# Two compressions taken in turn with projections, and half of an output projection held back over a change of halves

## The chip, the cores and the metric
The kernel runs on one core of a Trainium2 chip. The metric is the device time of one execution in microseconds (us). In the texts PE is TensorE, DVE is VectorE, ACT is ScalarE, POOL is GpSimd and SP is SyncE, whose queue issues the DMAs.

## The reference, cut to what matters
One decoder layer over 1024 tokens of width 1024, in float32. After an RMS norm one projection gives inputs for two mixers, whose outputs are concatenated, projected and added to x. A SwiGLU network (width 2816) and a last norm follow.
```python
z = h @ w_in
a_conv, q, kc_r, vc_r, ks, vs, kw, vw, g = jnp.split(z, splits, axis=-1)
conv_out = conv_mixer(a_conv, ...)          # gate, causal depthwise conv of width 31, norm, silu
kc = compress(kc_r, cmp_k_pe, cmp_k_w1, cmp_k_w2)
vc = compress(vc_r, cmp_v_pe, cmp_v_w1, cmp_v_w2)
nsa_out = nsa_attention(q, kc, vc, ks, vs, kw, vw, gates)   # compressed, chosen and window branch
x = x + jnp.concatenate([conv_out, nsa_out], -1) @ w_out
...
# compress: 32 rows of 64 make one block (stride 16), through w1 (2048 x 256), silu, w2 (256 x 64)
```

## The kernel before
Every product keeps float32 accuracy with three passes: each operand is split into a high part (cast to float32r) and a low part (the rest), and high x high, high x low and low x high are summed. `load_w` brings 512 KB of weights (DMA to `raw`, two buffers), lets ACT cast the high part and makes the low part in four pieces on POOL, or in one on DVE where it is called with `dve`; three buffers each hold high and low parts. `Feed` calls such loads two ahead of the one in use. `split` makes high and low of a result with ACT and DVE.

The order of the work is written by hand with generators. A generator yields estimated PE time after each product (0.216 a product of 512 columns, 0.117 to 0.12 of 264 or 274), and other generators are due by that time:

- The first part (`Drive`) runs over the first half of the tokens (0 to 511): `conv_in`, `compress_in` of the keys (two chunks of columns), q0 and q1 (`project_d`), `compress` of the keys (four chunks of `w1`, 24 products each), q2 to q5, `values` for the window branch, `compress_in` of the values, kw0 and ks0, `compress` of the values, kw1, `compress_v`, ks1. Beside it run side generators: `late_rows` (norm and transposes of row tiles 4 to 7), `tables` on POOL, `taps_in` (62 conv taps on DVE, two a step), `conv_tail`, and `stages_in(g)` (two compressed-attention stages `cmp_stage` for each of four groups, whose gaps are 5.0, 0.7, 10.0 and 0). `acc_bank` takes the banks of PSUM in turn by the string in `turn[1]`. `drive.run` takes the first FIRST_B = 48 items of the fill, and `drive.rest` issues what the sides still have.
- Then `weave` puts attention (main) and a fill together: for each unit of main, `RATIO_B` units of fill in the first half of attention (query tiles 0 to 3) and `RATIO_C` = 1.6 in the second. The fill `fill_b` holds the projections of the second half of the tokens, conv's last; then comes the output projection of set 0 in two parts (`kq`, each 512 rows of the mixed width, read back from `mix_d`), the norm, and products of the SwiGLU network (`ffn`). A yield of LEAD_C = 8 or MIXLAT = 6 gives the fill nothing to issue for that long; -1 means that it waits for main. `mixed(0, kq)` tells when attention has written that part.
- At last `second` does the output projection of set 1 (`out_proj_k`), beside more fill, and the remaining `ffn` passes end the program.

Instructions of one engine run in order, in an order that the framework makes of the traced one.

Of the kernel before, what the change touches and what calls it, by code (L numbers as in the profile page):

```python
# [19 lines left out]
P = 128  # L20
# [39 lines left out]


SLOPES = _slopes(HEADS)
RATIO_B = 0.9
RATIO_C = 1.6
RATIO_D = 1.3
LEAD_C = 8.0
# [22 lines left out]
def tile_hymba(ctx: ExitStack, tc, x, attn_norm, w_in, conv_w, conv_b, conv_ln_g, conv_ln_b,  # L89
# [186 lines left out]
    def win_chunk(c0):  # L276
        return load_w([(0, w_in[0, :, c0:c0 + P])], KT, P)
# [66 lines left out]
    def late_rows():  # L344
        for t in range(4, 8):
            with tc.issue_after(rows_in[0].ins), tc.issue_after(rows_in[1].ins):
                late[:] = [norm_rows(xts[t], xts[t], grow, pa, a4("junk"))]
            yield 2.4
            transpose_tile(xts[t], hhi[1], hlo[1], (t % 4) * P)

    rows = a4("rows")[:, :P]
# [76 lines left out]
            for i, z in ((0, zh), (1, zl)):  # L428
                sp.dma_start(dst[i, row:row + P, hf * 512:(hf + 1) * 512], z.bitcast(F32))

    def compress_in(ws, pe_col, out):
        xh = pa.tile([P, 8, GROUPS, 68], F32R, tag="xc", name="xh", bufs=2)
        xl = pa.tile([P, 8, GROUPS, 68], F32R, tag="xc", name="xl", bufs=2)
        for X in (xh, xl):
            pool.memset(X[:, :, :, 64:68].bitcast(F32), 0.0)
        for s in range(2):
            split(xh[:, :, 0, 64 + s], xl[:, :, 0, 64 + s], cols[:, pe_col + 8 * s:pe_col + 8 * s + 8])
        for hf in range(2):
            for m in range(2):
# [12 lines left out]
    def compress(xh, xl, w1, w2, tag, out):  # L452
        w1f = w1[0].rearrange("l d h -> (l d) h")
        hs = [bank("h0", tag), bank("h1", tag)]
        n = 0
        for jc in range(4):
            wh, wl = load_w([(0, w1f[jc * 512:(jc + 1) * 512, :])], 4, 256, dve)
            if jc == 1:
                w2r = pa.tile([P, 2, HD], F32, tag="w2r", name="w2r")
                pool.tensor_copy(w2r[:, 0, 0:1], wh[:, 0, 0:1].bitcast(F32))  # L460
            for j4 in range(4):
                j, s = (jc * 4 + j4) % 8, jc // 2
                for a, b in ((wh, xh), (wl, xh), (wh, xl)):
                    for ht in range(2):
                        mm(hs[ht][:, :264], a[:, j4, ht * P:(ht + 1) * P], b[:, j, :, s:s + 66],
                           start=n < 2, stop=n >= 94)
# [411 lines left out]
    def taps_in(n):  # L878
        taps = conv_taps(0)
        for _ in taps:  # L880
            yield n

    drive = Drive()
    xk, xv, kk, kv = [], [], [], []
    turn[1] = ACCS1
    drive.side(late_rows())
    drive.run(conv_in(first, 0))
    drive.side(tables(late[0], 3.0))
    drive.side(taps_in(2.2))
    drive.run(compress_in([win_chunk(C_KC + m * P) for m in range(2)], 68, xk))  # L890
    feed = Feed([q_load(m) for m in range(2)])
    for m in range(2):
        drive.run(project_d(feed, q_d, m * P, (0,), True))
    drive.run(compress(*xk, cmp_k_w1, cmp_k_w2, "s", kk))
    turn[1] = ACCS2
    feed = Feed([q_load(m) for m in range(2, 6)])
    for m in range(2, 6):
        drive.run(project_d(feed, q_d, m * P, (0,), True))
        if m == 2:
            compress_k(*kk)  # L900
            drive.side(stages_in(0), drive.t + 4.0)
        if m == 5:
            drive.side(stages_in(1))
    drive.run(values(Feed(value_loads(C_VW, 18)), 18, vw_d, 0))
    drive.side(stages_in(2))
    drive.run(compress_in([win_chunk(C_VC + m * P) for m in range(2)], 84, xv))
    drive.side(conv_tail(0))
    feed = Feed(kv_loads())
    for dst in (kw_d, ks_d):
        drive.run(project_d(feed, dst, 0, (0,)))  # L910
    drive.side(stages_in(3))
    drive.run(compress(*xv, cmp_v_w1, cmp_v_w2, "z", kv))
    turn[0] = -1
    for dst in (kw_d, ks_d):
        drive.run(project_d(feed, dst, P, (0,)))
        if dst is kw_d:
            compress_v(*kv)
    p2_stack.close()
    pa_stack.close()

# [80 lines left out]
    def set_in(si, p):  # L1001
        acts[si] = p
        pairs = [p.tile([P, 2, DM], F32, tag="x1", name="x1", bufs=2) for _ in range(2)]
        x1s[si] = [pairs[j // 2][:, j % 2, :] for j in range(4)]
        for t, x1 in zip(SETS[si], x1s[si]):
            sp.dma_start(x1, x[0, t * P:(t + 1) * P, :])

    def set_norm(si, p):
        pools[si] = p
        h2[si] = [[p.tile([P, 4, 512], F32R, name=f"h2_{si}_{w}_{j}") for j in range(2)] for w in range(2)]  # L1010
# [5 lines left out]
    def mix_in(si, kq):  # L1016
        assert mixed(si, kq)
        t0, n = SETS[si][0] * P, len(SETS[si]) * P
        mix = [acts[si].tile([P, 4, n], F32R, tag="act", name="mix", bufs=2) for _ in range(2)]
        for w in range(2):  # L1020
            sp.dma_start(mix[w].bitcast(F32),
                         mix_d[w, kq * 512:(kq + 1) * 512, t0:t0 + n].rearrange("(k p) t -> p k t", p=P))
        return mix

    def out_proj(feed, si, tags, kqs):
        for kq in kqs:
            mix = mix_in(si, kq)
            yield MIXLAT
            for ch in range(2):
                ws = [feed.get(), feed.get(1)]  # L1030
                for t, x1 in enumerate(x1s[si]):
                    o = bank("wo", tags[t % len(tags)])
                    n = 0
                    for k in range(4):
                        wh, wl = ws[k // 2]
                        for a, b in ((0, wh), (0, wl), (1, wh)):
                            pe.matmul(o, mix[a][:, k, t * P:(t + 1) * P], b[:, k % 2, :], start=n == 0, stop=n == 11)  # L1037
                            n += 1
                            yield MM
                    xs = x1[:, ch * 512:(ch + 1) * 512]  # L1040
                    dve.tensor_tensor(xs, o, xs, op=ALU.add)


    def out_proj_k(feed, si, tags):
        for kq in range(2):
            mix = mix_in(si, kq)
            feed.ahead(feed.n + 2)
            yield 0.0 if kq == 0 else MIXLAT
            for ch in range(2):
                os = [bank("wo", tags[t % len(tags)]) for t in range(len(x1s[si]))]  # L1050
# [100 lines left out]

    def fill_all():
        yield from fill_b()
        for kq in range(2):
            while not mixed(0, kq):
                yield -1.0
            if kq == 0:
                set_in(0, pm)
            else:
                p1_stack.close()  # L1160
                last["p3"], p = open_pool("p3", "left")
                set_norm(0, p)
            yield LEAD_C
            yield from out_proj(feed, 0, "z", (kq,))
        yield from ffn_norm_in(0, "z")
        while early[0] >= 0 and early[0] < NF // 2:
            early[0] += 1
            yield from ffn(feed, (0,), "z")
# [71 lines left out]
```

## Time and profile before
| | us |
|---|---|
| median of 3 runs (lowest to highest) | 1520.09 (1519.88 to 1520.77) |
| the profiled execution | 1518.21 |
| its span, first to last instruction | 1516.5 |
| PE, DVE, ACT, POOL busy in it | 1450.9, 824.9, 721.0, 816.6 |

Durations come from the profiled execution, whose span is its time less what lies around it. Busy is the time in which an engine has an instruction running; matmuls overlap, so that the sum of their durations is more than PE's busy time.

### The profile page before, as it was taken

To read this page: it belongs to the slowest core of one execution; us is meant where nothing else is said; L and a number is where in the kernel's file an instruction comes from. 1 tells how busy PE (TensorE), PEld (TensorE's weight loads), DVE (VectorE), ACT (ScalarE), POOL (GpSimd) and SP (SyncE) were. 2 spreads that over 40 slices of the span, in tenths; PEclk is the share of its full clock that TensorE was granted. 3 is DMA by queue.
4 is the path that set the end of the run, shared out by engine and by line. 5 is a ranking of instruction groups with operands and counts; after the bars stand their busy time and mean duration, and the time that the engine had idled before them with its cause. 6 is when DMAs were issued, how large, how long until landed. Compare 5 with 4: busy or idle time off the path is not lost.

```text
span 1516.5 us, 21864 instructions
## 1 busy us (share of the span) xinstructions
PE 1450.9 (96%) x7271; PEld 1217.2 (80%) x7271; DVE 824.9 (54%) x1936; ACT 721.0 (48%) x1468; POOL 816.6 (54%) x1156
## 2 busy tenths in 40 slices
PE   7989989999889889999999999999999999999997
PEld 6778779877768778888888877878788888888886
DVE  6994654667677686776677764223325222222323
ACT  6235655767766476666665654123212222222223
POOL 5626534757576455655664656445532545555554
PEclk9999999999999999999999999999999999999999
DMA  7237567666486362353353225433222322333332
GB/s 239 72 109 209 163 190 213 182 185 190 111 275 181 107 154 76 84 135 92 91 138 97 60 76 171 160 126 104 84 83 97 110 85 89 106 94 93 93 96 84
DMA packets 228717, 193.61 MB, mean 128 GB/s; under 512 B 15496, under 2 KB 197612, under 8 KB 228604
## 3 DMA queue, kind: packets, MB, share of 16 engines
q1 hardware_dynamic: 228604, 192.21, 43.0%
q8 instruction: 58, 0.95, 0.3%
q14 instruction: 55, 0.45, 0.1%
HBM read 158.42 MB, written 33.75 MB: 127 GB/s over the span
## 4 chain that ended last, share of the span: by engine, by line
PE 81%; DVE 7%; DMA 5%; ACT 4%; issue 2%; POOL 1%; SPq 0%; DVEq 0%; POOLq 0%; ACTq 0%
PE gu L1094 31%; PE dn L1114 15%; PE pt L783 5%; PE zo L145 4%; PE wo L1037 3%; PE vo L145 3%; PE wo L1055 3%; DVE cacc L553 3%; PE o L801 3%; DMA w_raw<-in_w_in_dram 2%; PE o L800 2%; PE s L756 2%; PE h L145 2%; DMA mix<-mix_d 1%; PE s L760 1%
## 5 line engine op out<-in xcount | busy, mean ns | idle before, releaser
L229 POOL TENSOR_TENSOR w_lo<-w_raw,w_hi 128x256 fp32r<-128x256 f32 (+1 forms) x688 | 526.8, 800 | 382.8 <-ACT w_hi L225 373.8
L1094 PE MATMUL gu<-h,w_hi 128*128 128x512 f32 x1408 | 454.4, 396 | 0.1
L225 ACT CAST w_hi<-w_raw 128x1024 fp32r<-128x1024 f32 (+1 forms) x182 | 190.4, 1050 | 389.6 <-PE gu L1094 166.9
L1094 PEld LDWEIGHTS gu<-h,w_hi 128*128 128x128 f32 x1408 | 263.1, 188 | 57.7 <-DVE h L233 0.4
L1094 PE MATMUL gu<-h,w_lo 128*128 128x512 f32 x704 | 278.8, 396 | 0.0
L1114 PE MATMUL dn<-w_hi,aw 128*128 128x512 f32 x704 | 234.8, 398 | 4.9 <-DVE af L1101 1.8
L777 POOL TENSOR_SCALAR pr<-pr,l,gates 128x640 f32<-128x640 f32 (+5 forms) x192 | 150.2, 798 | 125.0 <-DVE l L772 97.4
L1101 DVE TENSOR_TENSOR af<-gu,af 128x512 f32<-128x512 f32 x44 | 30.3, 690 | 287.4 <-PE gu L1094 204.9
L767 ACT ACTIVATE pr<-pr,m 128x640 f32<-128x640 f32 (+5 forms) x192 | 141.5, 738 | 93.5 <-DVE m L764 84.3
L1119 DVE TENSOR_TENSOR x<-dn,x 128x512 f32<-128x512 f32 x176 | 114.3, 684 | 94.2 <-PE dn L1114 93.9
L1114 PEld LDWEIGHTS dn<-w_hi,aw 128*128 128x128 f32 x704 | 131.8, 188 | 37.6 <-DVE af L1101 3.3
L233 DVE TENSOR_TENSOR pl<-pt,ph 128x384 fp32r<-128x384 f32 x264 | 141.7, 551 | 37.1 <-ACT ph L233 35.1
L1094 PEld LDWEIGHTS gu<-h,w_lo 128*128 128x128 f32 x704 | 132.2, 188 | 28.8
L233 ACT CAST ph<-pt 128x384 fp32r<-128x384 f32 x264 | 119.3, 478 | 74.6 <-PE pt L783 65.0
L783 PE MATMUL pt<-ident,pr 128*128 128x128 f32 x792 | 135.9, 276 | 3.3 <-DVE pl L233 2.5
L1114 PE MATMUL dn<-w_lo,aw 128*128 128x512 f32 x352 | 138.6, 394 | 0.0
L764 DVE CUSTOM_DVE_ANT_0 pr<-s,base 128x384 f32<-128x384 f32 (+3 forms) x192 | 101.4, 533 | 48.3 <-PE s L760 35.7
L783 PEld LDWEIGHTS pt<-ident,pr 128*128 128x128 f32 x792 | 102.3, 142 | 19.2 <-issue 2.6
L145 PE MATMUL zo<-h,w_hi 128*128 128x512 f32 x320 | 105.8, 400 | 4.0 <-ACT w_hi L225 2.6
L756 PE MATMUL s<-kt,q 128*128 128x384 f32 (+3 forms) x288 | 101.2, 353 | 1.5 <-DVE m L764 0.7
L800 PE MATMUL o<-ph,vt 128*128 128x384 f32 x264 | 98.3, 372 | 1.4 <-ACT ph L233 1.3
L801 PE MATMUL o<-pl,vt 128*128 128x384 f32 x264 | 93.4, 354 | 4.0 <-DVE pl L233 4.0
(207 smaller groups left out, 2320.9 us busy)
## 6 DMA issues: line engine op xcount, KB each, us to landing
w_raw<-in_w_gate_up_dram SPq DMA_DIRECT2D x84, 512.0 KB, 3.9
w_raw<-in_w_down_dram SPq DMA_DIRECT2D x42, 512.0 KB, 3.3
w_raw<-in_w_in_dram SPq DMA_DIRECT2D x40, 512.0 KB, 4.6
mix<-mix_d SPq DMA_DIRECT2D x8, 1024.0 KB, 6.7
q<-q_d SPq DMA_DIRECT2D x80, 96.0 KB, 3.1
qc<-q_d SPq DMA_DIRECT2D x32, 192.0 KB, 4.2
pc_d<-pct SPq DMA_DIRECT2D x16, 384.0 KB, 3.8
pct<-pc_d SPq DMA_DIRECT2D x32, 192.0 KB, 3.4
```

The source lines that it names most:

```text
L145: lastpe[0] = pe.matmul(*args, **kw)
L225: act.copy(hi[:, :n], raw[:, :n])
L229: eng.tensor_sub(lo[:, q], raw[:, q], hi[:, q].bitcast(F32))
L233: return act.copy(hi, src), dve.tensor_sub(lo, src, hi.bitcast(F32))
L756: pe.matmul(sv, q2[:, 0, r, :], kk_[:, 0, kk], start=True, stop=False)
L767: act.activation(pr[:, :n], pr[:, :n], AF.Exp, bias=m, scale=-1.0, accum_out=l3[:, r:r + 1])
L777: pool.tensor_scalar(x_, x_, l3[:, r2:r2 + 1], gates[:, i, c:c + 1], op0=ALU.mult, op1=ALU.mult)
L783: pe.transpose(pt[:, r * P:(r + 1) * P], prs[st][1 + r][:, kk * P:(kk + 1) * P], ident)
L800: pe.matmul(o[:, :384], v, ph, start=False, stop=False)
L801: pe.matmul(o[:, :384], v, pl, start=False, stop=last)
L1094: pe.matmul(o, w[:, k, :], h2[si][h][k // 4][:, k % 4, :], start=n == 0, stop=n == 3 * KT - 1)
L1114: pe.matmul(o, aws[si][:, a, k, t * P:(t + 1) * P], b[:, 0, ch * 512:(ch + 1) * 512], start=n == 0, stop=n == 5)
```

## The change
Eight things are edited. (1) One feed, `first`, serves the whole first part. (2) `compress` takes its chunks from that feed, with low parts on POOL instead of DVE. (3) The order is: `compress_in` of the keys, `values`, `compress` of the keys with q0 to q3 in turn after each chunk, q4, `compress_k`, q5, `compress_in` of the values, kw0, `compress` of the values with ks0 and kw1 after its first two chunks, ks1, `compress_v`. (4) Stages 0 to 3 start after q4, after `compress_in` of the values, after kw0 and after `compress` of the values; the sums of the projections from there on take "t" banks. (5) `late_rows` yields 4.0 instead of 2.4, `taps_in` 2.7 instead of 2.2. (6) RATIO_B is 0.82 instead of 0.9. (7) The output projection of set 0 asks for `mix` before the rows of x, in six pieces; of its first part the second half of the columns (48 products) is done after the second part's `mix` has been asked for. (8) In `out_proj_k` the loads of `mix` come in pieces too, and the x rows after them, in halves.
```diff
-RATIO_B = 0.9
+RATIO_B = 0.82
...
-            yield 2.4
+            yield 4.0
             transpose_tile(xts[t], hhi[1], hlo[1], (t % 4) * P)
...
-    def compress_in(ws, pe_col, out):
+    def compress_in(feed, pe_col, out):
+        ws = [feed.get(), feed.get(1)]
...
-            wh, wl = load_w([(0, w1f[jc * 512:(jc + 1) * 512, :])], 4, 256, dve)
+            wh, wl = feed.get()
...
+    def in_turn(main, others, part):
+        others = iter(others)
+        for n, d in enumerate(main):
+            yield d
+            if n % part == part - 1:
+                yield from next(others, ())
+        for o in others:
+            yield from o
...
+    def mixed_in(a, b):
+        return [ld for pair in itertools.zip_longest(a, b) for ld in pair if ld]
+
+    kvl = kv_loads()
+    first.loads += ([lambda m=m: win_chunk(C_KC + m * P) for m in range(2)] + value_loads(C_VW, 18)
+                    + mixed_in(w1_loads(cmp_k_w1), [q_load(m) for m in range(4)]) + [q_load(4), q_load(5)]
+                    + [lambda m=m: win_chunk(C_VC + m * P) for m in range(2)] + kvl[:1]
+                    + mixed_in(w1_loads(cmp_v_w1), kvl[1:3]) + kvl[3:])
...
-    drive.side(taps_in(2.2))
-    drive.run(compress_in([win_chunk(C_KC + m * P) for m in range(2)], 68, xk))
...
+    drive.side(taps_in(2.7))
+    drive.run(compress_in(first, 68, xk))
+    drive.run(values(first, 18, vw_d, 0))
+    drive.run(in_turn(compress(*xk, first, cmp_k_w2, "s", kk),
+                      [project_d(first, q_d, m * P, (0,), True) for m in range(4)], 24))
     turn[1] = ACCS2
...
+    drive.run(project_d(first, q_d, 4 * P, (0,), True))
+    compress_k(*kk)
+    drive.side(stages_in(0), drive.t + 4.0)
+    drive.run(project_d(first, q_d, 5 * P, (0,), True))
+    drive.run(compress_in(first, 84, xv))
+    drive.side(stages_in(1))
+    drive.run(project_d(first, kw_d, 0, (0,)))
+    drive.side(conv_tail(0), drive.t + 10.0)
     drive.side(stages_in(2))
...
+    turn[1] = "t"
+    drive.run(in_turn(compress(*xv, first, cmp_v_w2, "z", kv),
+                      [project_d(first, dst, r, (0,)) for dst, r in ((ks_d, 0), (kw_d, P))], 24))
     drive.side(stages_in(3))
...
+    drive.run(project_d(first, ks_d, P, (0,)))
+    compress_v(*kv)
...
-        for w in range(2):
-            sp.dma_start(mix[w].bitcast(F32),
-                         mix_d[w, kq * 512:(kq + 1) * 512, t0:t0 + n].rearrange("(k p) t -> p k t", p=P))
+        mix = [p.tile([P, 4, n], F32R, tag=tag, name="mix", bufs=2) for _ in range(2)]
+        src = [mix_d[w, kq * 512:(kq + 1) * 512, t0:t0 + n].rearrange("(k p) t -> p k t", p=P) for w in range(2)]
+        for a, b in ((0, 1), (1, 2), (2, 4)):
+            for w in range(2):
+                if tokens:
+                    sp.dma_start(mix[w][:, :, a * P:b * P].bitcast(F32), src[w][:, :, a * P:b * P])
+                else:
+                    sp.dma_start(mix[w][:, a:b, :].bitcast(F32), src[w][:, a:b, :])
...
-            mix = mix_in(si, kq)
+            mix = mix_in(si, kq, acts[si], tokens=False)
             feed.ahead(feed.n + 2)
+            if kq == 0:
+                x_in(si, 0)
+                x_in(si, 1)
...
-        for kq in range(2):
-            while not mixed(0, kq):
-                yield -1.0
-            if kq == 0:
-                set_in(0, pm)
-            else:
-                p1_stack.close()
-                last["p3"], p = open_pool("p3", "left")
-                set_norm(0, p)
-            yield LEAD_C
-            yield from out_proj(feed, 0, "z", (kq,))
+        while not mixed(0, 0):
+            yield -1.0
+        mix = mix_in(0, 0, pm)
+        set_in(0, pm)
+        x_in(0, 0)
+        x_in(0, 1)
+        yield LEAD_C
+        yield from out_proj(feed, 0, "z", mix, 0)
+
+        while not mixed(0, 1):
+            yield -1.0
+        p1_stack.close()
+        last["p3"], p = open_pool("p3", "left")
+        mix2 = mix_in(0, 1, p, "h21")
+        yield from out_proj(feed, 0, "z", mix, 1)
+        yield MIXLAT
+        for ch in range(2):
+            yield from out_proj(feed, 0, "z", mix2, ch)
+        set_norm(0, p)
```

## Rows read from the trace of the kernel before
**Rows 1.** Busy time by stretches: us, then each engine's busy time and instructions, clock, DMA.
```profile
core 0: us, PE busy (x) PEld busy (x) DVE busy (x) ACT busy (x) POOL busy (x), PEclk, DMA share, GB/s
58.00:91.00 33.00, 33.00 (x144) 26.68 (x143) 32.39 (x50) 9.82 (x19) 12.13 (x12) 1.00 0.18 50
91.00:104.00 13.00, 7.38 (x34) 6.60 (x33) 11.49 (x18) 3.33 (x7) 0.00 (x0) 0.74 0.54 177
104.00:187.00 83.00, 83.00 (x465) 72.06 (x464) 50.18 (x118) 47.20 (x133) 47.03 (x63) 1.00 0.63 181
187.00:229.00 42.00, 35.07 (x211) 30.60 (x209) 23.55 (x53) 23.99 (x55) 14.65 (x20) 0.96 0.62 185
326.00:429.00 103.00, 89.75 (x483) 74.40 (x484) 74.00 (x265) 76.85 (x216) 65.65 (x106) 0.97 0.61 170
429.00:448.00 19.00, 15.40 (x70) 12.63 (x69) 13.45 (x43) 12.14 (x44) 12.07 (x19) 0.91 0.98 340
478.00:504.00 26.00, 21.29 (x122) 18.14 (x121) 17.81 (x61) 16.63 (x37) 13.03 (x17) 0.93 0.69 201
560.00:1517.00 957.00, 941.78 (x4456) 777.87 (x4454) 435.31 (x898) 387.01 (x628) 506.13 (x689) 1.00 0.34 101
```
**Rows 2.** PE's timeline: start, length, instruction, idle before it and what ended that.
```profile
40.59 1.98 PE L248 MATMUL tp<-ident,xt 128*128 128x128 f32 x12 [2.85 <-DVE h L233]
...
96.91 0.81 PE L145 MATMUL h<-xh,w_hi 128*128 128x264 f32 x2 [5.08 <-ACT xh L233]
...
189.13 0.68 PE L145 MATMUL h<-xh,w_hi 128*128 128x264 f32 x2 [1.59 <-ACT w_hi L225]
...
437.83 0.76 PE L1037 MATMUL wo<-w_hi,mix 128*128 128x512 f32 x1 [3.16 <-DMA mix<-mix_d]
...
499.09 0.69 PE L1037 MATMUL wo<-w_hi,mix 128*128 128x512 f32 x1 [4.31 <-DMA mix<-mix_d]
```
**Rows 3.** Busy time by stretches at half clock, the longest and a short one.
```profile
96.50:103.30 6.80, 5.84 (x25) 5.54 (x26) 6.07 (x10) 1.98 (x3) 0.00 (x0) 0.50 0.53 178
499.20:502.60 3.40, 3.40 (x11) 2.83 (x12) 0.82 (x4) 0.48 (x1) 0.00 (x0) 0.51 1.06 298
```
**Rows 4.** The chain of waits in order of time: start, length, piece.
```profile
112.49 6.26 PE zo L145 x27
...
136.19 5.11 PE vo L145 x40
...
429.82 7.87 DMA mix<-mix_d
...
491.65 7.40 DMA mix<-mix_d
```
**Rows 5.** Groups of instructions in 58 to 104: busy us, mean ns, idle before.
```profile
L553 DVE SCALAR_TENSOR_TENSOR cacc<-y,cols,cacc 128x512 f32<-128x512 f32 x41 | 32.4, 819 | 0.3
...
L229 POOL TENSOR_TENSOR w_lo<-w_raw,w_hi 128x256 fp32r<-128x256 f32 x9 | 10.9, 1233 | 13.1 <-ACT w_hi L225 13.1
...
L233 ACT CAST xh<-zc 64x256 fp32r<-64x256 f32 x16 | 5.9, 367 | 24.7 <-DVE xl L233 20.3 <-PE zc L145 4.4
L229 DVE TENSOR_TENSOR w_lo<-w_raw,w_hi 128x1024 fp32r<-128x1024 f32 x3 | 3.6, 1212 | 0.0
```
**Rows 6.** POOL's timeline: a chunk's four pieces beside conv taps, and without.
```profile
79.54 5.62 POOL L229 TENSOR_TENSOR w_lo<-w_raw,w_hi 128x256 fp32r<-128x256 f32 x4 [13.15 <-ACT w_hi L225]
...
170.80 2.82 POOL L229 TENSOR_TENSOR w_lo<-w_raw,w_hi 128x256 fp32r<-128x256 f32 x4 [2.98 <-ACT w_hi L225]
```
**Rows 7.** DMA issues by kind: count, KB each, median us to landing.
```profile
w_raw<-in_w_in_dram SPq DMA_DIRECT2D x40, 512.0 KB, 4.6
```
**Rows 8.** Who PE waited for in 326 to 429: us, times, longest.
```profile
PE cv L145 <- ACT w_hi L225: 5.1, 3, 2.6
```
**Rows 9.** DVE's timeline: a row multiply, and conv taps.
```profile
32.01 7.28 DVE L241 SCALAR_TENSOR_TENSOR xt<-xt,rs,grow 128x1024 f32<-128x1024 f32 x1
...
62.23 6.69 DVE L553 SCALAR_TENSOR_TENSOR cacc<-y,cols,cacc 128x512 f32<-128x512 f32 x7
...
72.86 1.40 DVE L553 SCALAR_TENSOR_TENSOR cacc<-y,cols,cacc 128x512 f32<-128x512 f32 x2
```

More of the change, by code (lines that the diff above doesn't have):

```diff
@@ L450, in compress_in, with compress @@
         out.extend((xh, xl))
-    def compress(xh, xl, w1, w2, tag, out):
-        w1f = w1[0].rearrange("l d h -> (l d) h")
+    def compress(xh, xl, feed, w2, tag, out):
         hs = [bank("h0", tag), bank("h1", tag)]
@@ L881, in taps_in, with w1_loads @@
             yield n
+    def in_turn(main, others, part):
[6 more added lines that the diff above has]
+            yield from o
+    def w1_loads(w1):
+        w1f = w1[0].rearrange("l d h -> (l d) h")
+        return [lambda jc=jc: load_w([(0, w1f[jc * 512:(jc + 1) * 512, :])], 4, 256) for jc in range(4)]
+    def mixed_in(a, b):
[5 more added lines that the diff above has]
+                    + mixed_in(w1_loads(cmp_v_w1), kvl[1:3]) + kvl[3:])
     drive = Drive()
@@ L888, in tile_hymba @@
     drive.side(tables(late[0], 3.0))
-    drive.side(taps_in(2.2))
-    drive.run(compress_in([win_chunk(C_KC + m * P) for m in range(2)], 68, xk))
[L891 to L894, printed above, removed]
-    turn[1] = ACCS2
[L896 to L904, printed above, removed]
-    drive.side(stages_in(2))
[L906 to L910, printed above, removed]
-    drive.side(stages_in(3))
[L912 to L917, printed above, removed]
+    drive.side(taps_in(2.7))
[3 more added lines that the diff above has]
+                      [project_d(first, q_d, m * P, (0,), True) for m in range(4)], 24))
+    turn[1] = ACCS2
+    drive.run(project_d(first, q_d, 4 * P, (0,), True))
[6 more added lines that the diff above has]
+    drive.side(conv_tail(0), drive.t + 10.0)
+    drive.side(stages_in(2))
+    turn[1] = "t"
+    drive.run(in_turn(compress(*xv, first, cmp_v_w2, "z", kv),
+                      [project_d(first, dst, r, (0,)) for dst, r in ((ks_d, 0), (kw_d, P))], 24))
+    drive.side(stages_in(3))
+    drive.run(project_d(first, ks_d, P, (0,)))
+    compress_v(*kv)
     p2_stack.close()
@@ L1004, in set_in, with x_in @@
         x1s[si] = [pairs[j // 2][:, j % 2, :] for j in range(4)]
+    def x_in(si, ch):
+        h = slice(ch * 512, (ch + 1) * 512)
         for t, x1 in zip(SETS[si], x1s[si]):
-            sp.dma_start(x1, x[0, t * P:(t + 1) * P, :])
+            sp.dma_start(x1[:, h], x[0, t * P:(t + 1) * P, h])
     def set_norm(si, p):
         pools[si] = p
-        h2[si] = [[p.tile([P, 4, 512], F32R, name=f"h2_{si}_{w}_{j}") for j in range(2)] for w in range(2)]
+        h2[si] = [[p.tile([P, 4, 512], F32R, tag=f"h2{w}", name="h2", bufs=2) for _ in range(2)] for w in range(2)]
@@ L1013, in mixed, with mix_in @@
     def mixed(si, kq):
         return ("conv", si) in done and all(("mix", g, i) in done for g in range((2, GROUPS)[kq]) for i in SETS[si])
-    def mix_in(si, kq):
+    def mix_in(si, kq, p, tag="act", tokens=True):
         assert mixed(si, kq)
         t0, n = SETS[si][0] * P, len(SETS[si]) * P
-        mix = [acts[si].tile([P, 4, n], F32R, tag="act", name="mix", bufs=2) for _ in range(2)]
-        for w in range(2):
-            sp.dma_start(mix[w].bitcast(F32),
-                         mix_d[w, kq * 512:(kq + 1) * 512, t0:t0 + n].rearrange("(k p) t -> p k t", p=P))
-        return mix
@@ L1025, in out_proj @@
-    def out_proj(feed, si, tags, kqs):
-        for kq in kqs:
-            mix = mix_in(si, kq)
[L1028 to L1041, printed above, removed]
+        mix = [p.tile([P, 4, n], F32R, tag=tag, name="mix", bufs=2) for _ in range(2)]
@@ new lines, in mix_in, with out_proj @@
+        src = [mix_d[w, kq * 512:(kq + 1) * 512, t0:t0 + n].rearrange("(k p) t -> p k t", p=P) for w in range(2)]
[5 more added lines that the diff above has]
+                    sp.dma_start(mix[w][:, a:b, :].bitcast(F32), src[w][:, a:b, :])
+        return mix
+    def out_proj(feed, si, tags, mix, ch):
+        ws = [feed.get(), feed.get(1)]
+        for t, x1 in enumerate(x1s[si]):
+            o = bank("wo", tags[t % len(tags)])
+            n = 0
+            for k in range(4):
+                wh, wl = ws[k // 2]
+                for a, b in ((0, wh), (0, wl), (1, wh)):
+                    pe.matmul(o, mix[a][:, k, t * P:(t + 1) * P], b[:, k % 2, :], start=n == 0, stop=n == 11)
+                    n += 1
+                    yield MM
+            xs = x1[:, ch * 512:(ch + 1) * 512]
+            dve.tensor_tensor(xs, o, xs, op=ALU.add)
@@ L1044, in out_proj_k @@
     def out_proj_k(feed, si, tags):
         for kq in range(2):
-            mix = mix_in(si, kq)
+            mix = mix_in(si, kq, acts[si], tokens=False)
             feed.ahead(feed.n + 2)
+            if kq == 0:
+                x_in(si, 0)
+                x_in(si, 1)
             yield 0.0 if kq == 0 else MIXLAT
```

## The prediction
> **What bounds the kernel now.** I read the table by stretches first [rows 1]: TensorE (PE) is busy nearly all the time, every other engine far less, and the diff does not change PE's work. So the time can move only through PE's idle stretches (window minus busy) and through stretches at a lower clock. From 560 us to the end 957 us hold only 15 us of idle time, while 91 to 104 hold 5.62, 187 to 229 hold 6.93, 326 to 429 hold 13.25, 429 to 448 hold 3.60 and 478 to 504 hold 4.71. Next I asked PE's timeline what ended the long ones [rows 2]: a transpose waits for VectorE (DVE) at 40.59; the key compression for its input at 96.91; the value compression for a weight cast at 189.13 (the first of six short waits up to 204); the output projection twice for `mix`, 3.16 and 4.31 us. Last the granted clock [rows 3]: after idle like these it is at half, the lower of its two levels (1.2 GHz of 2.4), once for 6.8 and seven times for 3.4 us. At half clock 3.4 us do the work of 1.7, so such a wait costs its length plus 1.7 (plus 2.9 behind the key compression: 6.80 us less the 0.96 idle in it, halved).
>
> **Term 1, the key compression.** Between `compress_in` and `compress`, q0 and q1 (48 products of 0.232 us, by 27 in 6.26 [rows 4], 11.1 us) give way to `values` (96 of 0.128, by 40 in 5.11, 12.3 us): the cover for the splits that write `xh` and `xl` is about the same. What changes is DVE. In 58 to 91 it was busy 32.39 of 33 us [rows 1], most of it with conv taps, 41 of 819 ns in 58 to 104; ScalarE (ACT) stood 20.3 us waiting for low splits queued between taps [rows 5]. So DVE, not a load, set the 5.08 us wait. Taps every 2.7 units instead of 2.2 are 33 instead of 41 here, 6 us of DVE less, some 5 of them ahead of the last split; and two of three low parts of 1.21 us that DVE made for `compress` stood ahead of it too and go to GpSimd (POOL). That is 7 us off a queue that was 5 us late: I expect this wait to go. Removed: 5.62 + 2.9 = 8.5 us. What replaces it: compression chunks of 24 products (at the rate of `values` 3.0 us) alternate with projections of 5.6, so a pair of weight chunks has 8.6 us. On POOL a chunk is four pieces: 2.82 us alone, 5.62 beside taps [rows 6], 4 x 1.233 = 4.9 there on average [rows 5]. Two take 5.6 to 9.8 us. At 9.8 the four pairs fall 4 x 1.2 = 4.8 us behind, less a lead of one or two chunks made during `values`; at 5.6 nothing. Loads keep up, 4.6 us each with two buffers [rows 7], and one feed now asks two chunks ahead across all these steps where separate feeds began anew. I take 2.5 us of new waiting: -6.0; ends 0 (POOL costs all of it) and -8.5.
>
> **Term 2, the value compression.** Chunk after chunk without other products, 3.0 us of work met a chain of load, cast and DVE low part; it loses 6.93 + 1.7 = 8.6 us. After, two of its chunks are followed by a projection, the last two by none. No taps run here any more, so POOL's chunk is 2.82 us: a pair has time, the last two are about level. The projections' sums now share three "t" banks with the conv tail and the stage transposes, and a wait on one stops PE in its order, with every product behind it; stages 1 and 2 also come closer together. I take 3.1 us of new waiting: -5.5; ends 0 and -8.6.
>
> **Term 3, the change between the halves.** Before, `fill_all` gives nothing for 8 + 6 units of its time (LEAD_C, MIXLAT) at each of two `mix` loads, in which PE has attention alone; idle 3.60 + 4.71, clock 2 x 1.7, sum 11.7. At the first, the chain of waits shows the load running 7.87 us from 429.82, when its buffers (the second half's `h`) are nearly free, to the wait's end [rows 4]; both 1 MB tiles must land whole. After, it is asked for ahead of the x rows, and the two pieces of 128 columns (512 KB together, a quarter) let the first products start; 8 units stand between instead of 6. At the second, 48 held-back products (11.1 us) plus attention's own run while 7.40 us of load pass [rows 4], and the pause after them is 6 units, not 14. Costs: SP issues 14 transfers instead of 6 around the first load, and attention's `q` and `kt` loads stand behind them; the x rows now follow `mix` and are needed after 12 products, the "z" banks held until then. The 10.4 units that move into the second half find ffn products without end behind them, so they cost nothing there. The new order in `out_proj_k` has cover, since the part from 560 on idles little. I take 2.7 us of new waiting: -9.0; ends -4 and -11.7.
>
> **Term 4, RATIO_B.** Fill of 0.82 instead of 0.9 per unit of attention spreads the products longer. In 326 to 429 conv products wait 5.1 us for weight casts [rows 8], which a slower demand relieves; against it, attention's own waits get less cover, and conv's last products end later, past the change of halves. The stretch's 13.25 us are far from either; I bound it by -6 and +4 and take -1.
>
> **Term 5, late_rows.** 4.0 instead of 2.4 puts each row tile's transposes some 7 products later. The wait of 2.85 + 1.7 = 4.5 us stands behind a DVE multiply of 7.28 us [rows 9], which may recur. Ends -4.5 and 0; I take -1.
>
> **Term 6, what is pushed out.** Stage 3 now starts after the value compression, with one projection (5.2 units) and FIRST_B (10.4) before `drive.rest()`; it wants 2 x 15.7 by its gaps. So its second half is issued without spacing at attention's start: a load, six score products, ACT's exponentials and a transpose, in the order of their engines. A load alone is some 4.6 us [rows 7]. Ends 0 and +6; I take +2, as other products stand beside it.
>
> Sum: -6.0 - 5.5 - 9.0 - 1 - 1 + 2 = -20.5 us. The profiled execution took 1518.21 us (span 1516.5), 1.9 under the median of 1520.09. 1518.2 - 20.5 = 1497.7 there, **1499.6 us** as a median.
>
> **A rule against it.** Taps and POOL's pieces delay each other in rows: seven taps beside a train of pieces took 6.69 us (0.96 each), two elsewhere 1.40 (0.70), so 1.8 us of DVE a train; and the multiply of 7.28 us, twice a tap's length, is 5.9 us over two taps' 1.40 [rows 9]. The Trainium skill, "SBUF — State Buffer", section "Who interferes with whom", says that a DVE instruction with two SBUF inputs contends with a GpSimd instruction that reads SBUF, and that the second to issue is blocked until the first is done. The rows agree that they delay one another; by the page the low parts that move to POOL are not free for the taps, and the sum would lean to rival B.
>
> **Rivals.**
> A, POOL becomes the feeder: at 4.9 us a chunk or more both compressions still wait, terms 1 and 2 go to 0. 1499.6 + 11.5 = 1511. For it: 5.62 us for one chunk [rows 6]; against: the taps are over by the value part. 12 in 100.
> B, slower: DVE starves. In units of the order, 35 steps of taps now last until the value projections: 16 chunks of POOL fall on them (kc 2, vw 2, w1 4, q 6, vc 2), before 10. At 5.9 us each, less the 1.8 already there, that is 94 - 18 = 76 us; DVE's idle time in 58 to 187 is 34.9 us [rows 1], plus 4 x 1.2 that leave it, 39.7. The 36 us over end as waits of PE for splits: 1499.6 + 36 = 1536. It turns slower from (39.7 + 18 + 23.5) / 16 = 5.1 us a chunk; the taps' row says 1.8. 8 in 100.
> C, the change of halves keeps its waits: `mix` cannot be asked for before conv's last products, which come later, and its pieces with the x rows crowd out attention's loads. Term 3 goes to 0: 1508.6. For it: DMA is at 0.98 in 429 to 448 [rows 1]. 8 in 100.
> D, the edit works and terms 4 and 5 come in too: 1490 or less, 1481 with the ends of all. 8 in 100.
> The forecast as such, 1490 to 1508: 64 in 100.
>
> **The numbers.** 0.2% is 3 us, about what a measurement of this kernel can tell. A, C, D and the forecast are faster by more; A and C together (1520) are not. Faster 86, same 6, slower 8 in 100. The range takes in the forecast, C, A and most of D: 1486 to 1514, leaving out some 6 below and 14 above.
>
> **What would show it.** Right: no PE wait above 2 us between the end of `compress_in` and that of `compress`, twice; none on `mix`; full clock through these; attention starting some 10 us earlier; DVE in the taps' time clearly under 98% busy. Term 1 wrong: PE waits on POOL's `w_lo` or on `xh` there. Term 2: on `cl`, `cn` or "t" banks. Term 3: `wo` still ended by `mix`, or attention's products by `kt` or `q`. Term 6: waits for `pg` or `sc` behind FIRST_B. The forecast as a whole fails if DVE is full again, or if the idle time of 326 to 429 grows.

## The result, and the profile after
The changed kernel takes 1501.86 us (median of 4 runs, 1499.39 to 1503.15) against 1519.99 us (1518.91 to 1520.77) for the kernel before beside it: ratio 0.9877, 95% interval 0.9853 to 0.9901. The forecast was 1499.6 us. The profiled span went from 1516.5 to 1497.7 us, 18.8 less. The time is as forecast. Its terms are only partly so, and the runs below show that much of the gain hangs on something that the prediction did not price.

Busy time by stretches, of the changed kernel, with the columns of [rows 1]:
```profile
56.78:89.00 32.22, 31.65 (x167) 27.02 (x166) 31.55 (x50) 9.44 (x21) 16.77 (x18) 1.00 0.20 53
89.00:96.00 7.00, 4.83 (x27) 4.33 (x26) 6.84 (x16) 1.46 (x4) 0.00 (x0) 0.76 0.42 150
96.00:177.00 81.00, 80.26 (x401) 67.09 (x400) 37.93 (x71) 36.98 (x78) 50.18 (x67) 1.00 0.57 163
177.00:203.00 26.00, 24.68 (x169) 22.59 (x167) 15.00 (x41) 15.59 (x43) 17.16 (x25) 1.00 0.66 194
203.00:217.00 14.00, 9.18 (x30) 7.18 (x31) 6.94 (x20) 13.86 (x37) 8.01 (x11) 0.76 0.78 208
317.00:424.00 107.00, 100.70 (x538) 82.57 (x537) 82.66 (x286) 80.97 (x228) 71.84 (x115) 0.98 0.65 183
424.00:436.00 12.00, 9.37 (x34) 7.56 (x33) 7.59 (x20) 7.80 (x32) 10.27 (x16) 0.72 1.00 322
474.00:495.00 21.00, 18.22 (x98) 15.64 (x98) 12.14 (x36) 9.62 (x23) 6.73 (x8) 0.92 0.83 231
```
The idle time of 5.62 us ahead of the key compression is 2.17 (89 to 96). That of the value compression, 6.93, is nearly as large as before: 1.32 (177 to 203) and 4.82 (203 to 217, clock 0.76). At the change of the halves 3.60 and 4.71 became 2.63 and 2.78. In the first half of attention, ahead of conv's last product, 13.25 us in 103 (326 to 429) became 6.30 in 107 (317 to 424). VectorE (DVE) is as full as before in the taps' time, 31.55 of 32.22 us.

PE's timeline of the changed kernel shows what ended these waits:
```profile
91.18 0.68 PE L145 MATMUL h<-xh,w_hi 128*128 128x264 f32 x2 [1.74 <-ACT xh L233]
...
205.56 0.41 PE L582 MATMUL cm<-ident,cn 128*128 128x128 f32 x2 [2.67 <-DVE cl L626]
...
208.45 0.79 PE L145 MATMUL zo<-h,w_hi 128*128 128x512 f32 x1 [2.26 <-ACT af L475]
...
427.63 0.50 PE L1055 MATMUL wo<-w_hi,mix 128*128 128x512 f32 x1 [1.43 <-DVE y L530]
...
476.11 0.51 PE L1055 MATMUL wo<-w_hi,mix 128*128 128x512 f32 x1 [1.89 <-DMA mix<-mix_d]
...
492.12 0.50 PE L1055 MATMUL wo<-w_hi,mix 128*128 128x512 f32 x1 [0.89 <-DMA mix<-mix_d]
```
Against [rows 2]: the key compression's wait is 1.74 us instead of 5.08, those on `mix` 1.89 and 0.89 instead of 3.16 and 4.31. The weight-cast waits of the value compression gave way to two others, a transpose of the conv tail (`cm`, L582) and a projection's product (`zo`), which `compress`'s silu `af` ended. The first output product, at 425.52, no longer waits for `mix`, but a later one waits 1.43 us for VectorE's product `y`, which reads a sum of conv's.

The stretches at half clock after, busy time by stretches:
```profile
91.40:94.80 3.40, 2.97 (x13) 2.69 (x13) 3.27 (x7) 0.37 (x1) 0.00 (x0) 0.50 0.22 82
207.40:214.20 6.80, 5.75 (x14) 4.49 (x15) 4.40 (x11) 6.74 (x19) 6.27 (x9) 0.50 0.49 130
429.30:436.10 6.80, 6.04 (x17) 5.22 (x17) 4.05 (x10) 3.03 (x15) 6.29 (x10) 0.50 1.06 360
477.10:480.50 3.40, 3.40 (x9) 2.72 (x9) 0.00 (x0) 0.00 (x0) 0.01 (x1) 0.50 1.15 318
```
With one more of 3.4 us at 357.6 these are all up to 1490 us, 23.8 us together; before there were one of 6.8 and seven of 3.4 [rows 3], 30.6 us together. A second execution of the changed kernel (`after_again`, below) took nearly the same time with 30.6 us of half clock, at partly other places.

**The ledger.** To compare kernels whose orders differ I add up, over all PE instructions, how much later the next one starts than the first quartile for that shape in the kernel before. That is "time lost": idle, half clock and small delays. Milestones that all kernels share cut it into stages, headed by the prediction's terms: 5, up to `compress_in` of the keys; 1, up to that of the values; 2, the rest of the first part; 6, the 48 products of FIRST_B; 4, attention up to conv's last product; 3, from there to the first ffn product; "att", the rest of attention; "rest", from the last score product to the end, with `out_proj_k` in it. One profiled execution each, us:
```
kernel             5     1     2     6     4     3   att  rest    sum
before          22.3  11.3  16.3   0.3  51.1  41.1  35.9  21.1  199.4
after           20.8   7.5  15.1   1.7  47.5  30.2  41.2  16.7  180.7
after_again     21.7   7.4  15.3   3.6  44.9  30.5  41.1  16.8  181.4
first_only      21.9   5.6  15.9   6.3  53.9  41.1  40.7  22.2  207.6
halves_only     21.5  11.4  18.6   0.3  48.8  30.2  41.1  17.8  189.7
ratio_only      21.1  11.4  18.3   0.3  62.7  44.2  33.4  18.0  209.4
halves_ratio    22.2  11.0  16.3   0.3  65.5  34.2  36.5  25.6  211.6
first_ratio     21.7   6.3  14.8   6.3  46.6  44.6  37.9  23.4  201.7
after_ratio09   22.2   7.3  15.1   8.4  56.6  37.5  42.2  17.7  207.0
after_ratio086  22.0   5.8  15.1   3.7  52.1  28.5  41.6  28.0  196.7
after_ratio081  21.3   6.9  16.5   3.7  50.1  32.6  42.9  24.8  198.8
after_w1_dve    21.6   6.5  10.6   2.0  59.9  41.4  35.4  25.5  202.8
tail_late       26.2   6.1   5.9   7.0  54.2  30.6  41.5  28.4  199.9
ratio09_poolq   22.0   5.8  15.1   3.6  54.8  28.4  49.4  29.7  208.8
```
The sum falls by 18.7 from before to after, which is the span's difference. Of `after_ratio09` the profiled execution was some 8 us above that kernel's median.

How much two rows can differ by chance can be read from the table, too. Up to 290 us PE, DVE, ACT and POOL run the same instructions in the same order in seven of these executions: `after`, `after_again`, `first_only`, `first_ratio` and the three in which the ratio alone is another. Stage 6 loses 1.7 to 8.4 us in them, and stages 5, 1, 2 and 6 together 45.1 to 53.0. A difference of that size between two rows is not by itself an effect of the text.

### The profile page after: what moved, and what is told of

Read it like the earlier page. It is cut to its first block, busy times and chain, and to the rows that moved or that the text cites. A ratio compares the mean times of both kernels' runs of the same rounds, so it can differ in the third digit from the quotient of the medians.

```text
span 1497.7 us, 21904 instructions
## 1 busy us (share of the span) xinstructions
PE 1447.7 (97%) x7271; PEld 1214.5 (81%) x7271; DVE 818.4 (55%) x1928; ACT 730.4 (49%) x1477; POOL 839.1 (56%) x1188
## 4 chain that ended last, share of the span: by engine, by line
PE 66%; DVE 4%; DMA 4%; ACT 2%; POOL 2%; issue 1%; SPq 0%; DVEq 0%; POOLq 0%; ACTq 0%
PE gu L1115 30%; PE dn L1135 15%; PE pt L783 4%; PE wo L1055 3%; PE s L756 2%; PE o L801 2%; PE o L800 2%; PE wo L1076 2%; PE s L760 1%; PE s L758 1%; DMA w_raw<-in_w_in_dram 1%; DMA mix<-mix_d 1%; DMA o_raw<-in_w_out_dram 1%; PE cv L145 1%; DVE pl L233 1%
## 5 line engine op out<-in xcount | busy, mean ns | idle before, releaser
L229 POOL TENSOR_TENSOR w_lo<-w_raw,w_hi 128x256 fp32r<-128x256 f32 (+1 forms) x720 | 550.9, 800 | 359.5 <-ACT w_hi L225 346.6
L1115 PEld LDWEIGHTS gu<-h,w_hi 128*128 128x128 f32 x1408 | 263.4, 188 | 56.6
L145 PE MATMUL zo<-h,w_hi 128*128 128x512 f32 x320 | 108.9, 408 | 4.0 <-ACT af L475 2.3
```

The lines of the kernel that those rows point to most:

```text
L145: lastpe[0] = pe.matmul(*args, **kw)
L229: eng.tensor_sub(lo[:, q], raw[:, q], hi[:, q].bitcast(F32))
L1115: pe.matmul(o, w[:, k, :], h2[si][h][k // 4][:, k % 4, :], start=n == 0, stop=n == 3 * KT - 1)
```

## The experiments
The theory at the start was the prediction's: three separate places, each with its own price. The rivals were that one of them carries it all, or that the pace (RATIO_B) does.

**The parts alone.** `first_only` has the new first part, with the old `set_in`, `out_proj` and `fill_all`, and 0.9; `halves_only` has the new ones with the old first part and 0.9; `after_ratio09` has both with 0.9.
```diff
first_only, after_ratio09 (against after; first_only also with the old out_proj and fill_all)
-RATIO_B = 0.82
+RATIO_B = 0.9
halves_only (against before)
+        mix = mix_in(0, 0, pm)
...
+        mix2 = mix_in(0, 1, p, "h21")
```


> The new first part alone: the second half's fill, the output projection and RATIO_B = 0.9 are those of before. Theory (each place gives what its own waits cost): up to the end of the first part PE lost 49.9 us in the kernel before and 43.4 after the change, so about 1514 us. Rival 1 (the first part carries nearly all, because attention starts on other footing): 1505 or less. Rival 2 (what it gains is lost again where attention starts): 1518 to 1522.

> The change of halves alone: pieces of mix, mix ahead of the x rows, the held-back half and the new order in out_proj_k, with the first part of before and RATIO_B = 0.9. Theory: the waits of 3.16 and 4.31 us on mix and their two stretches at half clock shrink to 2 us or less in all, 1509 to 1512 us. Rival (mix cannot come before conv's last product, and its pieces crowd attention's loads): no gain, 1517 to 1522, wo still ended by mix.

> The changed kernel with RATIO_B = 0.9 again. Theory (the ratio is a small term): 1502 to 1506 us, with the idle time of attention's first half a few us more. Rival 1 (the thinner fill is what opens attention's first half, and the rest gains little): 1510 or more. Rival 2 (a thinner fill only costs cover): 1497 to 1500.

Measured: `first_only` 1528.57 us, ratio 1.0057 (1.0039 to 1.0075), slower than any of its expectations; `halves_only` 1509.48, 0.9923 (0.9896 to 0.9950); `after_ratio09` 1517.97, 0.9987 (0.9964 to 1.0010), in the range of its rival 1. So the change of halves alone gives the time that was expected, but not in the way that its theory had: the waits on `mix` there are 4.9 us, where 2 or less were expected.
```profile
PE wo L1041 <- DMA mix<-mix_d: 4.9, 2, 3.0
```
The first part alone costs time, although it loses 5.7 us less in stage 1: it loses 6.0 more in FIRST_B, of which much is chance by the spread above, and 7.6 more in attention, stages 4 and "att". And the pace, priced at 1 us, seemed to be worth 16.

**The low parts of `w1`.** `after_w1_dve` gives them back to DVE.
```diff
-    return [lambda jc=jc: load_w([(0, w1f[jc * 512:(jc + 1) * 512, :])], 4, 256) for jc in range(4)]
+    return [lambda jc=jc: load_w([(0, w1f[jc * 512:(jc + 1) * 512, :])], 4, 256, dve) for jc in range(4)]
```


> The changed kernel with the low parts of the compressions' weights on VectorE again, 8 of 1.2 us. Theory (VectorE is full while the taps run): the splits before the key compression end later by the 1 to 2 low parts ahead of them, its wait of 1.7 us grows to 3 to 4, 1503 to 1507 us. Rival A (GpSimd's chunks beside taps, 4 to 5.6 us each, hold the compressions up): 1497 to 1500. Rival B (its trains starve VectorE): the taps end earlier by 5 us or more and the time falls.

Measured: 1522.4 us, ratio 1.0018 (0.9995 to 1.0040), above all three expectations. The place that was edited is better, not worse: stages 1 and 2 lose 17.1 us instead of 22.6 (20.9 to 23.4 in the seven executions of one order). But by attention's first score product, which waits 3.9 us for `q` here, it can no longer be told from chance: from the values' first `zc` product to there 17.7 us are lost, against 17.6 to 24.3 in those seven. What it loses beyond the changed kernel, 26.6 us, lies all behind FIRST_B, from some 230 us on, in code that is the same word for word.

**The pace by itself, and the text once more.**
```diff
after_again: no edit
ratio_only (before)
-RATIO_B = 0.9
+RATIO_B = 0.82
halves_ratio (halves_only)
-RATIO_B = 0.9
+RATIO_B = 0.82
after_ratio086 (after)
-RATIO_B = 0.82
+RATIO_B = 0.86
```


> The changed kernel once more, beside kernels that differ from it in one value. All theories: 1500 to 1504 us, if the kernel before stands at 1518 to 1520 here.

> The kernel before with RATIO_B = 0.82 and nothing else. Theory (the thinner fill is worth some 16 us in any company): 1502 to 1506 us. Rival 1 (it only pays together with the change of halves, since conv's last products then end past the end of the first half): 1516 to 1524. Rival 2 (it repairs what the new first part does to attention's start and gives nothing without it): 1516 to 1520.

> The change of halves and RATIO_B = 0.82 with the first part of before. If the three parts add (first part +10, halves -9, ratio -16): 1491 to 1496 us, faster than the whole change. Rival (the ratio repairs what the new first part does, and is worth little without it): 1506 to 1512.

> The changed kernel with RATIO_B = 0.86, between 0.82 (1502) and 0.9 (1518). If the ratio acts as a density of fill: in between, 1507 to 1513 us. Rival (each value gives another order of instructions, and the times scatter with the order, not with the density): outside of 1502 to 1518, or nearer to one end than 2 us.

Measured: `after_again` 1502.24 us, 0.9876 (0.9836 to 0.9915): the time belongs to this text. `ratio_only` 1530.75, 1.0073 (1.0053 to 1.0093), and `halves_ratio` 1535.47, 1.0093 (1.0058 to 1.0127), both slower than any value expected of them; `after_ratio086` 1517.02, 0.9978 (0.9957 to 1.0000), as its rival said. With the old first part 0.82 costs 11.6 and 16.7 us in stage 4; with the new one it is worth 7.3 (`first_only` to `first_ratio`) and 9.1 (`after_ratio09` to after). The medians agree in sign: 11 and 26 us slower, 8 and 16 us faster. No price for the pace alone exists.

**Three trials at the places in doubt.** `first_ratio` is the last corner of the eight combinations. `ratio09_poolq` tests whether weight loads that stand behind attention's transfers in SyncE's order make 0.9 slow: who PE waited for between 237 and 440 us in `after_ratio09` begins
```profile
PE zo L145 <- ACT w_hi L225: 5.8, 2, 3.7
PE s L756 <- DVE m L764: 3.5, 4, 2.5
```
`tail_late` tests what the two new waits of the value compression come from.
```diff
ratio09_poolq (after_ratio09), in load_w
-            sp.dma_start(v[:, :, c:c + src.shape[-1]], ...)
+            (pool if pace and phase[0] == 0 else sp).dma_start(v[:, :, c:c + src.shape[-1]], ...)
tail_late (after)
-    drive.side(conv_tail(0), drive.t + 10.0)
     drive.side(stages_in(2))
...
     drive.side(stages_in(3))
+    drive.side(conv_tail(0))
```


> The new first part with RATIO_B 0.82, the change between the halves as before: the one corner of the eight combinations of first part, halves and ratio that had not been run. Theory: the change between the halves is worth its 10 to 11 us of idle and half-clock time wherever it is put in, and the ratio pays with the new first part: 1502 + 10.5 = 1512 us (1509 to 1516), with the two waits for mix back, 3 us or more each, in the trace. Rival 1: the parts simply add as they did alone (first part +10, ratio +11): 1540 us. Rival 2: the ratio pays only where all three are together, because what it gains lies at the change of the halves: 1525 us or more, and then the time lost in the first half of attention is no less than the 57 us that it was with 0.9.

> The changed kernel with RATIO_B 0.9 (1518 us), and the weight loads of the first half of attention issued by GpSimd instead of SyncE, behind the marker copy that GpSimd makes for them anyway. Theory: what the ratio of 0.9 costs is weight loads that stand behind attention's own transfers in SyncE's order, so that 7.0 us of TensorE waits for casts (and the half clock after them) go: 1518 - 7 - 4 = 1507 us (1503 to 1511), and waits for w_hi between 240 and 430 us below 2 us. Rival 1: the loads are late because of the marker or of the transfer itself, not because of the queue: 1518 us (1514 to 1522), waits for w_hi still 4 us or more. Rival 2: GpSimd, which makes the low parts, falls behind with the issues: waits for w_lo instead, 1524 us or more.

> The changed kernel with the first conv tail put behind the value compression (after the start of stage 3) instead of before it. Theory: the waits that took the place of the removed ones in the value compression (2.7 us of cm on DVE, 2.3 of zo on ScalarE, and 6.8 us of half clock around them, together 6 to 8 us) come from the conv tail crossing stages 1 and 2 in the same engines' order and go with it: 1502 - 6 = 1496 us (1493 to 1499). Rival 1: they come from the stages alone and stay, or they move behind the value compression: 1502 us (1499 to 1505). Rival 2: the tail now runs into the start of attention together with stage 3, whose waits grow by more than is won: 1508 us or more.

Measured: `first_ratio` 1520.12 us, ratio 0.9993 (0.9979 to 1.0006). That is between theory and rival 2, and the sign that rival 2 named is not there: stage 4 loses 46.6 us, not 57. Of its 21.0 us over the changed kernel 14.4 are lost where the halves change, 4.6 in FIRST_B (chance, by the spread above) and 6.7 in the rest. This is the purest comparison of all: up to 430 us PE, DVE, ACT and POOL run the changed kernel's order, and what differs is edits (7) and (8). In this company they are worth 18 us, twice the forecast's 9.0. And stage 4 loses 44.9, 46.6 and 47.5 us in the three executions that share its order, so there the spread of one order is small. Who PE waited for in 427 to 552 begins with the old wait:
```profile
PE wo L1051 <- DMA mix<-mix_d: 5.5, 2, 3.4
```
`ratio09_poolq` 1530.28, 1.0059 (1.0041 to 1.0077): casts make PE wait 3.8 us instead of 7.0 between 240 and 434 us, yet stage 4 loses 54.8 us against 56.6. So SyncE's order is half of the cast waits, and taking it away did not bring stage 4 back. POOL's falling behind (rival 2) is not it either, though the time is in rival 2's range: PE's waits on `w_lo` there sum to 0.3 us, and what the run adds lies behind, in "att" (8.2 us over the changed kernel) and the rest (13.0), where the products of `out_proj_k` wait 7.1 us for weight casts.

`tail_late` 1519.12, 0.9989 (0.9971 to 1.0006). The first half of its theory holds; busy time by stretches of that run:
```profile
177.00:211.00 34.00, 33.23 (x205) 29.50 (x205) 17.81 (x50) 19.84 (x60) 22.84 (x32) 1.00 0.76 222
211.00:240.00 29.00, 27.32 (x153) 24.20 (x152) 19.12 (x50) 21.85 (x52) 17.33 (x25) 0.88 0.76 224
```
Through the value compression PE now idles 0.77 us at full clock, and stage 2 loses 5.9 us instead of 15.1: the two waits were the conv tail's, which crossed stages 1 and 2 in the order of PE, DVE and ACT. It holds a little further, too: up to attention's first score product 13.7 us are lost from the values' first `zc` on, against 17.6 to 24.3. The second half fails, and the time is in rival 2's range: FIRST_B loses 5.3 us more (7.0, within the spread above), stage 4 6.7 more, the rest 11.7 more. Who PE waited for from 885 us on in this run begins
```profile
PE wo L1076 <- DMA mix<-mix_d: 4.4, 1, 4.4
PE dn L1135 <- DVE aw L233: 1.6, 1, 1.6
PE dn L1135 <- DVE x L1140: 1.5, 1, 1.5
```
where the changed kernel has
```profile
PE wo L1076 <- DMA mix<-mix_d: 0.9, 1, 0.9
PE dn L1135 <- ACT aw L233: 0.8, 1, 0.8
```
The edit stands some 800 us earlier, and no instruction in between was changed, only the order.

**One hundredth of the pace.** Is 0.82 a pace that pays, or one favourable order?
```diff
-RATIO_B = 0.82
+RATIO_B = 0.81
```


> The changed kernel with RATIO_B 0.81 instead of 0.82, one hundredth, which as a pace is next to nothing (the fill of the first half of attention is asked for 1.2% later) but makes every engine's order from there on anew. Theory: the 15 us between 0.82 and its neighbours 0.86 and 0.9 are no effect of the pace; 0.82 is one favourable order among many, and every other change to the text so far landed at 1517 to 1530. So 0.81 gives 1517 us (1509 to 1527), with waits for weight casts, for mix or behind attention back at other places, and the removed waits of the key compression and the change of the halves still gone. Rival: the slower pace itself is what pays, from about 0.83 down; then 0.81 gives 1502 us (1498 to 1505) with less than 49 us lost up to the last conv product.

Measured: 1516.18 us (12 runs, 1506.81 to 1522.76), ratio 0.9962 (0.9944 to 0.9979). That is the number of the theory. Of the 18.1 us that its execution loses beyond the changed kernel's, 8.1 are in the rest, 2.6 in stage 4, 2.4 in the change of the halves, 2.0 in FIRST_B (where the order is still the same). A slower pace, then, is not what makes 0.82 fast.

## Why the prediction was right, and where it was not
The sum was -20.5 us and came out as -18.7, but the terms did not come out as worked. That the number fits is in good part luck, as the sum below shows.

**Term 1** (-6.0) measured -3.8. The mechanism is right. From the first `zc` product to the last low split it took 39.96 us before and 35.84 after; in it stood 38 conv taps with 30.1 us of DVE before, 33 with 25.7 after, and the two low parts of 1.21 us are gone. That is the 7 us of the working. But 2.5 us moved in that the term left out, as the groups on DVE in 56.78 to 92.62 of the changed kernel show:
```profile
L553 DVE SCALAR_TENSOR_TENSOR cacc<-y,cols,cacc 128x512 f32<-128x512 f32 x33 | 25.7, 807 | 0.3
...
L233 DVE TENSOR_TENSOR h<-tp,h 128x512 fp32r<-128x512 f32 x2 | 1.4, 676 | 0.0
...
L233 DVE TENSOR_TENSOR vv<-vo,vv 128x256 fp32r<-128x256 f32 x2 | 0.8, 420 | 0.0
```
They are `vv` from `values`, with 0.3 us of gates, and the `h` of the last row tile, which `late_rows` at 4.0 now brings there. So a wait of 1.74 us and a half clock of 3.4 stay (1.8 and 6.8 in the second execution). All new first parts lie between 5.6 and 7.5 against 11.0 to 11.4: this term adds up everywhere.

**Term 2** (-5.5) measured -1.2: the worst-sized of the terms that have a place of their own. The cast waits went, as worked, and neither the "t" banks nor a pair of chunks too slow for POOL took their place; the conv tail did, as `tail_late` shows, at 9.2 us of stage 2. I had named it only as a user of the banks. DVE's and ACT's timelines of the changed kernel show how it crosses the stages:
```profile
204.80 0.17 DVE L625 TENSOR_SCALAR cl<-cl 128x6 f32<-128x6 f32 x1 [3.50 <-ACT cs L623]
204.88 0.54 DVE L576 TENSOR_SCALAR cn<-cl,mv,crs 128x256 f32<-128x256 f32 x1
...
201.38 1.28 ACT L623 ACT_TABLE_LOAD   x1 [1.93 <-DVE bm L619]
...
206.63 1.28 ACT L475 ACT_TABLE_LOAD   x1
207.93 0.47 ACT L475 ACTIVATE af<-h,bc 128x256 f32<-128x256 f32 x1
```
The tail's `cn`, for which PE's `cm` waits, stands on DVE behind a stage's `cl`, and that waits 3.5 us for the stage's exponentials. ACT loads a table of 1.28 us ahead of these (L623), and another ahead of the silu `af` that PE's `zo` waits for (L475). From the values' first `zc` product to attention's first score product it loads 10 tables here, 4 before, and 6 each in `tail_late` and `after_w1_dve`, the two runs in which stage 2 loses less. That the loads are the reason was not tested by itself. Nor is a price of the chunks on POOL shown: with `w1` on DVE stage 2 loses 10.6 us instead of 15.1, but in the changed kernel no wait of PE there ends with a `w_lo`.

**Term 3** (-9.0) measured -10.9 up to the first ffn product, and 5.3 of it comes back in "att". The stretch holds 23 us less than before (113.2 instead of 136.6), so some of attention, with its small delays, now stands behind it. Stages 3 and "att" together, with and without the edit, in the four pairs: -5.7, -6.9, -2.1 and, for the full change, -11.1; on average -6.5. By the whole times of the same pairs it is -9, +5, -11 and -18 us. What all runs show is the idle time: in stage 3 PE idles 7.1 to 10.6 us in the ten executions with the edit and 12.6 to 13.7 in the four without. The waits for `mix` are less sure: 7.5 us before and 2.8 here, but 5.0 in the second execution, up to 7.1 in the others with the edit, and 2.2 to 6.8 in the others without. So the mechanism came in part. What the term had wrong besides is the clock: at the first `mix`, two short waits for DVE (1.43 and 0.43 us) are followed by 6.8 us at half clock, where 3.4 stood before, so that the whole stretch still has 10.2 us of it, as before (6.8 in the second execution).

**Term 4** (-1, ends -6 and +4) measured -3.6 in the full change, but it is no term: +11.6 or +16.7 with the old first part, -7.3 or -9.1 with the new. The step of the prediction that failed is to cost the pace by itself from one stretch of the trace before.

**Term 5** (-1) measured -1.5 up to the key compression, and -0.6 in the second execution of the same text; the wait behind the row multiply recurred, 2.29 us at 42.03 and 7.32 us of multiply, where [rows 9] has 7.28. **Term 6** (+2) measured +1.4 and +3.3 in the two executions, and +4.5 on average in the seven of the same order. The part from the last score product on gave 4.4. Edit (8) acts in it, which term 3 had put at nothing, and rightly so: in `out_proj_k` 2.8 us were lost before, 1.6 and 2.7 in the two executions.

So the terms for the first part and the halves (1, 2, 3 with "att", 5, 6) came to -10.7 us, and to -7.6 in the second execution, of -19.5; -8.0 and -10.5 lay in stage 4 and the rest, where I had forecast -1. The new first part is the worst of it: terms 1, 2, 5 and 6 forecast -10.5 and measured -5.1, and over the seven executions of its order against the four with the old one it is 48.6 against 50.7 us lost, -2.1. `after_ratio086` has -10.5 in the places of these terms, next to the changed kernel's -10.7, and loses 7.9 more than before in stage 4 and the rest: 1517 us. That is the finding. In the eight runs with both the new first part and the new halves those places give -2.9 to -10.7 us (`after_ratio09` alone +5.5). Stage 4 and the rest, whose text differs between these runs at most in the pace and in who issues loads, lose from 61.7 (`after_again`) to 85.4 us (`after_w1_dve`), 72.2 before. The changed text stands at the good end of both, and nothing in the prediction's working could tell that it would.

**The rivals.** A: POOL is no bound of the key compression: from 55 to 145 us PE waits 0.9 us for `w_lo`, where 6.0 were to come back, and the 1.74 us that stay end with a split. In the value compression no wait of PE ends with it. The Trainium skill, "SBUF — State Buffer", section "Who interferes with whom", says that a DVE instruction with two SBUF inputs contends with a GpSimd instruction that reads SBUF. The trace agrees in kind: a chunk beside taps took 5.63 and 4.18 us, 2.82 where none run.
```profile
77.09 5.63 POOL L229 TENSOR_TENSOR w_lo<-w_raw,w_hi 128x274 fp32r<-128x274 f32 x4 [13.35 <-ACT w_hi L225]
83.13 4.18 POOL L229 TENSOR_TENSOR w_lo<-w_raw,w_hi 128x256 fp32r<-128x256 f32 x4 [0.41 <-ACT w_hi L225]
...
124.13 2.82 POOL L229 TENSOR_TENSOR w_lo<-w_raw,w_hi 128x256 fp32r<-128x256 f32 x4 [2.37 <-ACT w_hi L225]
```
B: DVE did not starve; from 96 to 177 us it was busy 37.93 of 81. Its sign that I gave for failure, DVE full again, was a bad one: DVE was full (98% of 56.78 to 89), with its backlog shorter. The other sign of failure, more idle time ahead of conv's last products, did not come. Attention starts 2.3 us earlier (239.75 to 237.49), not 10: term 2 did not come, and FIRST_B took 1.4 more. C: it came true in the clock, and in part in the waits on `mix`. D did not come.

**What stays open.** Why stage 4 loses 44.9 us with one text and 65.5 with another. Waits for casts are part of it (1.1 and 1.8 us in the two executions of the changed kernel, 7.7 before, 8.3 and 8.4 in `ratio_only` and `halves_ratio`), half clock another, but `ratio09_poolq` removed half of the one and gained nothing. That the order does it, and not chance, is shown: three executions of one order lie within 2.6 us, while `tail_late` and `after_w1_dve` lose 54.2 and 59.9 at the same pace. By which of its waits is not. It was not tried without the marker copy of `load_w`. No kernel here beats the changed one; `tail_late` shows 9 us in stage 2 that a better order further on might keep.

## What to carry to other kernels
Where a program orders instructions by due times, an edit has two prices: what it does where it stands, which rows of the trace can tell (here they gave about half of the forecast), and what the new order does to everything behind it, which they cannot: 0.81 against 0.82 moved 14 us. Test a constant at its neighbours before believing its gain, keep the two prices apart in a ledger by stage, and take the ledger's own spread from executions that share an order. When a wait is removed, look which other step crosses that place in the order of the same engines; here the conv tail was waiting to be next.

## What was not expected of the hardware
One and the same small instruction, in the same order and at the same place, took 0.71 us in one execution and 3.71 in another. DVE's timeline of the changed kernel:
```profile
40.07 0.71 DVE L304 TENSOR_SCALAR gates<-gates 128x72 f32<-128x72 f32 x1
40.82 0.60 DVE L305 RECIPROCAL gates<-gates 128x72 f32<-128x72 f32 x1
41.34 1.22 DVE L233 TENSOR_TENSOR h<-tp,h 128x512 fp32r<-128x512 f32 x2
```
and of `tail_late`, whose order is the same up to far behind this place:
```profile
39.95 3.71 DVE L304 TENSOR_SCALAR gates<-gates 128x72 f32<-128x72 f32 x1
43.70 0.60 DVE L305 RECIPROCAL gates<-gates 128x72 f32<-128x72 f32 x1
44.22 1.22 DVE L233 TENSOR_TENSOR h<-tp,h 128x512 fp32r<-128x512 f32 x2
```
PE's wait for that `h` was 5.3 us there instead of 2.3, and the clock went to half for 6.8 us, where in the changed kernel it stayed full: stage 5 lost 26.2 us instead of 20.8. In the second execution of the changed kernel the instruction took 1.27 us. What made it longer is not shown. A half clock behind one wait and not behind another makes such small differences large. Runs of one text also spread differently: the 8 of the changed kernel lie within 5.5 us, 12 of `after_ratio081` within 16.
